# A two-layer hybrid trunk on one core: three weight copies placed behind the last scaled row of the feed-forward stage

## The chip, the cores and the metric

The kernel runs on one core of one Trainium2 chip. The metric is the device time of one execution in microseconds (us), the median of several runs. The core has five engines that each work through their own queue in order: PE (TensorE, matrix products), DVE (VectorE) and ACT (ScalarE) for elementwise work, POOL (GpSimd), and SP (SyncE), which here only issues transfers. They wait for one another through semaphores.

## What is computed

Two decoder layers on 528 columns (16 meta tokens and 512 tokens) of width 1024. Cut to what matters here:

```python
xn = rmsnorm(h, attn_norm_g)
proj = jnp.einsum('bld,dc->blc', xn, w_in)
...
mix = jnp.concatenate([fox_out, ret_out], axis=-1)
h = h + jnp.einsum('blc,cd->bld', mix, w_out)

hn = rmsnorm(h, ffn_norm_g)
ff = jax.nn.silu(jnp.einsum('bld,df->blf', hn, w_gate)) * jnp.einsum('bld,df->blf', hn, w_up)
return h + jnp.einsum('blf,fd->bld', ff, w_down)
```

All inputs and the output are float32. The second layer needs only the 512 token columns from the output projection on.

## The kernel before

Activations lie transposed: 8 tiles `h[0]` to `h[7]` of 128 rows (model width) by 528 columns. To keep precision, every operand of a product is written as a sum of two rounded parts, a high part (`xh`, `whi`, `fwhi`) that ACT copies and a low part (`xl`, `wlo`, `fwlo`) that DVE (or POOL) makes by subtracting; PE then does three products, high by high, high weight by low operand, low weight by high operand.

Weights come as jobs in a list. A job has a raw buffer (`raw`, a ring of four), filled by a transfer that SP issues; `convert` makes its high and low parts in halves of 128x512, into the ring `whi`/`wlo` (two deep) or, in the feed-forward stage, also into `fwhi`/`fwlo` (three deep).

The place that matters is the passage from the output projection to the feed-forward stage, once in each layer. It is made of these steps:

- The second half of the output projection makes eight results, one for each `h[m]`, by PE into PSUM (`psd` is a ring of two, `psa` another of four). DVE adds each to `h[m]` (`add_h`, lines 837 and 840). Results 4 and 5 use weights in `rqh`, `rql`, `rkh`, `rkl`; results 6 and 7 use weights in `whi`/`wlo`. Result 6 can begin only when DVE has emptied the `psd` buffer of result 4.
- `start_ffn` calls `scale_split`: for each k, ACT writes `xh[k]` from `h[k]` (line 347, "a scaled row" below) and DVE writes `xl[k]` (line 349). `squares` has ACT square each `h[k]` into `sq` (lines 360 and 365) and DVE sum them into `ss` (line 369). The sum of squares is split (`sqh`, `sql`), summed over the partitions by PE with a matrix of ones (line 310) and turned into the factor `R` (lines 315 to 327).
- The feed-forward stage has 22 blocks of 128 hidden columns. Blocks 0 and 1 are "plain": four dense products, gate 0, up 0, gate 1, up 1 (`dense_steps`, line 229). Gate 0 and both up products write `psd`, gate 1 writes `psa`. Their results are scaled by `R` on DVE (lines 878, 881, 889). Blocks 2 to 21 are "units" (`Unit`): a fast scheme with seven half-size products in place of eight. Their weights are made by `make1` to `make4` (lines 934, 935), and their operands `th`, `tl` by `x_forms` (lines 907 to 911, 153).
- The first three jobs of the stage are converted ahead of it: `start_ring` converts gate 0, `more_ring(1)` up 0, `more_ring(2)` gate 1. Up 1 (`whi`/`wlo`) and the first product of block 2 (`make1`) are converted by the steps that look ahead.

PE's order is written out by hand. ACT's, DVE's and POOL's orders are made by a scheduler from the program's order and priorities; `tc.issue_after(ins)` puts what is traced in its block behind `ins` on that engine, and `pin` keeps the written order. `ff["after"]` holds such marks for the jobs of the plain blocks: a dictionary, the key behind which the high copy goes (`"gated"`, the last gated retention result), and the key behind which the low copy goes.

Of the kernel before, what the change touches and what calls it, by code (L numbers as in the profile page):

```python
# [16 lines left out]
NK = D // 128  # L17
# [10 lines left out]
PLAIN = 2  # L28
# [11 lines left out]
def hybrid_kernel(ctx, tc, x_t, w_in, w_fl, w_out, w_gate, w_up, w_down, vecs, b_fg, rope, decay, mask, ident, out_t):  # L40
# [34 lines left out]
    def enter(name, side="left"):  # L75
        if side in phase:
            old, cm = phase.pop(side)
            cm.__exit__(None, None, None)
            phase.pop(old)
        if name:  # L80
            cm = tc.tile_pool(name=name, bufs=1, side=side, reuse_waits="tile")
            phase[side] = name, cm
            phase[name] = cm.__enter__()
# [91 lines left out]
    def convert(j, upto=NK, pinned=False):  # L175

        if j >= len(jobs):
            return
        job = jobs[j]
        fetch(j)  # L180
        if "make" in job:
            if "w" not in job:
                n = job["n"]
                hi, lo = (wring(job["ring"] + p) for p in ("whi", "wlo"))
                job["w"] = [(NK, hi, lo)]
                job["make"](hi[:, 0:n], lo[:, 0:n])
            return
        n = job["src"].shape[1]
        if "w" not in job:
            job["w"] = job["own"]() if job["own"] else \  # L190
                [(NK, *[wring(i) for i in ("whi", "wlo")])]
            job["split"] = 0
        sub = nc.gpsimd.tensor_sub if job["pool"] else nc.vector.tensor_sub
        while job["split"] < min(n, upto):
            c0 = job["split"]
            c1 = min(n, c0 + (2 if j < 2 and c0 < 4 else 4))
            size, hi, lo = job["w"][c0 // job["w"][0][0]]
            o = c0 % size
            hi, lo = hi[:, o:o + c1 - c0], lo[:, o:o + c1 - c0]
            marks, after, before = job["after"] or (None, None, None)  # L200
            with tc.high_priority() if j == 5 else tc.issue_after(marks[after]) if after else ExitStack():
                pin(nc.scalar.copy(hi, job["raw"][:, c0:c1]), pinned)  # L202
            step = 1 if job["pool"] else c1 - c0
            with tc.issue_after(marks[before]) if before else ExitStack():
                for c in range(0, c1 - c0, step):
                    pin(sub(lo[:, c:c + step], job["raw"][:, c0 + c:c0 + c + step], hi[:, c:c + step].bitcast(F32)), pinned)  # L206
            job["split"] = c1

    def dense_steps(src, parts, pool=False, banks=False, ahead=(1, 4), own=None, wait=None, far=False, after=None):

        j = len(jobs)
        jobs.append({"src": src, "pool": pool, "own": own, "after": after})

        def chunk(k0, k, n, xs, cols, ps, done):
            def go():
                convert(j)
                if k == 0:
                    t = [psum_a() for _ in cols] if banks else psum()  # L220
                    ps.append(t)
                    ps.append(t if banks else [t[:, b] for b in range(2)])
                size = jobs[j]["w"][0][0]
                _, hi, lo = jobs[j]["w"][(k0 + k) // size]
                wk = (k0 + k) % size
                xh, xl = xs(k)
                for i, (w, x) in enumerate(((hi, xh), (hi, xl), (lo, xh))):
                    for b, (c0, c1) in enumerate(cols):
                        nc.tensor.matmul(ps[1][b][:, 0:c1 - c0], w[:, wk, :], x[:, c0:c1],  # L229
                                         start=(k == 0 and i == 0), stop=(k == n - 1 and i == 2))  # L230
                if k == n - 1:
                    done(ps[0]) if wait is None else wait.append((ps[0], done))
                for half, at_step in enumerate(ahead):
                    if k0 + k == at_step:
                        convert(j + 1, 4 * half + 4)
                        if far:
                            convert(j + 2, 4 * half + 4)
            return go

        steps = []  # L240
        for k0, xs, n, cols, done in parts:
            ps = []
            steps += [chunk(k0, k, n, xs, cols, ps, done) for k in range(n)]
        return steps
# [28 lines left out]
    def psum_a():  # L273
        return psa.tile([128, 512], F32, name="psa", tag="psa")
# [64 lines left out]
    def scale_split(st, gcol, cols, then=None):  # L339

        c = slice(cols[0][0], cols[-1][1])
        st["x"] = []
        for k in range(NK):
            xh = state.tile([128, T], F32R, name=f"xh{k}", tag=f"xh{k}")
            xl = state.tile([128, T], F32R, name=f"xl{k}", tag=f"xl{k}")
            g = vcol(gcol + k)
            st["scaled"] = nc.scalar.activation(xh[:, c], h[k][:, c], AF.Copy, scale=g)  # L347
            pin(st["scaled"], then)
            pin(nc.vector.scalar_tensor_tensor(xl[:, c], h[k][:, c], g, xh[:, c].bitcast(F32),  # L349
                                               ALU.mult, ALU.subtract), then)  # L350
            st["x"].append((xh, xl))
            if then and k in then:
                then[k]()

# [503 lines left out]
    def ffn(l, st, real, last):  # L858
        QC = REAL if real else FULL
# [3 lines left out]
        xs = lambda k: st["x"][k]  # L863
# [22 lines left out]
        def u_done(f):  # L886
            def go(ps):
                u = tt("tq")
                nc.vector.scalar_tensor_tensor(sv(u, real), pv(ps, real), RSC, sv(st["R"], real), ALU.mult, ALU.mult)
                nc.vector.tensor_mul(sv(u, real), sv(u, real), sv(sgs[f], real))  # L890
                fh, fl = act_tile(f)
                split(sv(fh, real), sv(fl, real), sv(u, real))
                acts[f] = (fh, fl)
            return go
# [38 lines left out]
        def splits(hi, lo, src):  # L933
            nc.scalar.copy(hi, src)  # L934
            nc.vector.tensor_sub(lo, src, hi.bitcast(F32))  # L935
# [17 lines left out]
        class Unit:  # L953
# [17 lines left out]


            def make1(self, hi, lo):
                splits(hi, lo, self.t["a"])


            def make2(self, hi, lo):
# [123 lines left out]
        steps = []  # L1101
        fills = []
        units = {}
        for r, (f0, f1) in enumerate(ROUNDS):
            for f in range(f0, f1):
                if f < PLAIN:
                    if f == 0:
                        st["first"] = range(len(jobs), len(jobs) + 3)
                    steps += dense_steps(w_gate[l, f], [(0, xs, NK, QC, g_done(f) if f else held.append)], banks=f == 1, own=own, far=f == 1, after=st["after"][2 * f])
                    steps += dense_steps(w_up[l, f], [(0, xs, NK, QC, u_done(f))], own=None if f else own, far=f == 0, after=None if f else st["after"][1])  # L1110
                    continue
                for i in (f, f + 1) if f == PLAIN else (f,):
                    if i not in units:
                        units[i] = Unit(i)
                        steps += units[i].head()
                u = units[f]
                u.rest()
                steps += u.middle()
                p, g0, g1 = fills.pop(0)
                j = down_job(p, g0, g1)  # L1120
                steps += down(j, 0, 2 * p, g0, g1, not real or f < PLAIN + 2)
                u.last()
                steps += u.tail()
                steps += down(j, 1, 2 * p + 1, g0, g1, f == PLAIN)
            fills = [(p, f0, f1) for p in range(NK // 2)]
# [172 lines left out]
    def layer(l):  # L1298

        real = l == DEPTH - 1  # L1300
        QC = REAL if real else FULL
        ly, ff = {"wait": []}, {}
        fox = [{} for _ in range(FP)]
        ret = [{} for _ in range(RH)]
# [17 lines left out]
        plan = []  # L1322
# [34 lines left out]
        def more_ring(i):  # L1357
            return lambda: convert(ff["first"][i])
# [25 lines left out]
        plan = [lambda: enter_att(l), start]  # L1384
# [11 lines left out]
        for g in range(2):  # L1396
# [6 lines left out]
        op = out_proj(l, 0, mixes[0], real)  # L1403
# [6 lines left out]
        op = out_proj(l, 1, mixes[1], real, marks)  # L1410
# [1 line left out]
        plan += merge(base, spread(main, 2, 46.5), spread(rest, 51, 56),  # L1412
                      ret_places(2, 26, 23.5, 24.5, 32, 28, 33.5, 36, 56.5, 40.5, 57.5),
                      ret_places(3, 52, 45.5, 47.5, 57.5, 54.9, 58.5, 60, 64.1, 63, 64.2))
        plan += [start_ring, op[3], op[7], op[11], op[15]] + op[16:28] + [more_ring(1)] + op[28:] + [more_ring(2)]
        ff["after"] = [(ret[3], "gated", x) for x in ("mixed", ("added", 6), ("added", 7))]
        up = ffn(l, ff, real, real)
        plan += [lambda: enter("ffn"), start_ffn] + up
        return plan

    plan = [f for l in range(DEPTH) for f in layer(l)]
# [76 lines left out]
```

## Time and profile before

| | |
|---|---|
| median of 3 runs | 1269.51 us (1269.06 to 1270.74) |
| the profiled execution | 1271.65 us |
| its span, first to last instruction | 1269.9 us |
| granted TensorE clock, mean | 0.994 of full speed |
| transfers | 116.21 MB, 92 GB/s on average |
| passage of layer 0 / of layer 1 | about 266 to 314 us / about 893 to 944 us |

The profile is of one execution. Row by row, its timeline gives start, duration, engine, line, operation, output and inputs, how many instructions were merged into the row (x2), and in brackets the time that the engine sat idle just before, with what ended it. [...]

### The profile page before, as it was taken

The numbers are of one execution on the slowest core, as the hardware profiler recorded it, in microseconds if no ns is written. First come the engines' busy times: TensorE is split into PE (matmuls) and PEld (weight loads), VectorE is DVE, ScalarE is ACT, GpSimd is POOL, SyncE is SP. The second block draws the span as 40 slices with busy tenths as digits, with TensorE's granted clock in tenths as the row PEclk, the third lists the DMA queues.
The fourth block names the chain that finished last, engine by engine and source line by source line (L and its number), as shares of the span: only waits on it lengthen the run. The fifth ranks groups of instructions, "written<-read, shape, count | busy, mean of one in ns | idle before, by whom it ended". The sixth has DMA issues, their size and how long they took to land.

```text
span 1269.9 us, 23673 instructions
## 1 busy us (share of the span) xinstructions
PE 1251.1 (99%) x9291; PEld 1197.2 (94%) x9291; DVE 993.0 (78%) x1801; ACT 709.7 (56%) x1317; POOL 294.6 (23%) x568
## 2 busy tenths in 40 slices
PE   9999999999999999999999999999899999999997
PEld 8999999999999999999999988998789999999997
DVE  7887756889997777777776776468899978888866
ACT  7767656775544444444466675567655444444444
POOL 4545655430000000000045556655200000000000
PEclk9999999999999999999999999999899999999999
DMA  6222223123332333332312222222314333333312
GB/s 234 68 76 76 68 68 92 51 85 99 116 103 99 100 101 100 100 100 67 117 60 83 76 76 84 67 76 67 124 51 132 109 100 100 100 100 106 111 51 67
DMA packets 43344, 116.21 MB, mean 92 GB/s; under 512 B 5089, under 2 KB 9953, under 8 KB 43233
## 3 DMA queue, kind: packets, MB, share of 16 engines
q1 hardware_dynamic: 42800, 114.41, 28.0%
q8 instruction: 73, 1.20, 0.4%
q14 instruction: 39, 0.31, 0.1%
q10 hardware_dynamic: 432, 0.29, 0.1%
HBM read 112.58 MB, written 2.10 MB: 90 GB/s over the span
## 4 chain that ended last, share of the span: by engine, by line
PE 86%; DVE 7%; ACT 2%; POOL 2%; issue 2%; DMA 1%; DVEq 0%; POOLq 0%; ACTq 0%; SPq 0%
PE psd L229 23%; PE psa L946 19%; PE psd L946 14%; PE psd L1087 13%; PE psa L1087 5%; PE psa L229 3%; PE psa L449 2%; PE psa L616 2%; PE psa L546 1%; PE psa L750 1%; PE psa L786 1%; DVE ss L369 1%; DMA raw<-w_gate 1%; POOL rkl L206 1%; ACT xh L347 0%
## 5 line engine op out<-in xcount | busy, mean ns | idle before, releaser
L206 POOL TENSOR_TENSOR wlo<-raw,whi 128x128 fp32r<-128x128 f32 x488 | 254.7, 557 | 212.6 <-ACT whi L202 195.6
L229 PE MATMUL psd<-xh,whi 128*128 128x264 f32 (+1 forms) x696 | 169.5, 313 | 0.3 <-ACT whi L202 0.3
L229 PE MATMUL psd<-xh,wlo 128*128 128x264 f32 (+1 forms) x696 | 160.7, 300 | 0.0
L229 PE MATMUL psd<-xl,whi 128*128 128x264 f32 (+1 forms) x696 | 160.5, 299 | 0.2 <-DVE xl L349 0.2
L934 ACT CAST fwhi<-raw 128x1024 fp32r<-128x1024 f32 (+1 forms) x64 | 56.8, 889 | 108.3 <-PE psa L946 65.3
L229 PEld LDWEIGHTS psd<-xh,whi 128*128 128x128 f32 x696 | 112.1, 189 | 3.8 <-ACT whi L202 0.8
L229 PEld LDWEIGHTS psd<-xh,wlo 128*128 128x128 f32 x696 | 110.9, 188 | 4.4
L229 PEld LDWEIGHTS psd<-xl,whi 128*128 128x128 f32 x696 | 111.4, 188 | 3.0 <-DVE xl L349 0.4
L202 ACT CAST whi<-raw 128x512 fp32r<-128x512 f32 (+1 forms) x140 | 82.2, 612 | 32.8 <-PE psd L229 17.0
L125 POOL MEMSET kc<- 64x528 f32 x4 | 2.1, 534 | 377.2 <-PE psd L1087 377.1
L935 DVE TENSOR_TENSOR fwlo<-raw,fwhi 128x1024 fp32r<-128x1024 f32 (+1 forms) x64 | 65.2, 1018 | 30.6 <-ACT fwhi L934 30.6
L934 ACT CAST whi<-raw 128x1024 fp32r<-128x1024 f32 (+1 forms) x64 | 57.0, 890 | 43.5 <-PE psd L946 39.4
L935 DVE TENSOR_TENSOR wlo<-raw,whi 128x1024 fp32r<-128x1024 f32 (+1 forms) x64 | 65.2, 1019 | 8.1 <-ACT whi L934 8.1
L946 PE MATMUL psa<-tl,fwhi 128*128 128x264 f32 (+1 forms) x248 | 70.2, 283 | 0.0
L946 PE MATMUL psa<-th,fwhi 128*128 128x264 f32 (+1 forms) x248 | 70.2, 283 | 0.0
L946 PE MATMUL psa<-th,fwlo 128*128 128x264 f32 (+1 forms) x248 | 70.1, 283 | 0.0
L1014 ACT COPY e<-psa 128x264 f32<-128x264 f32 (+1 forms) x120 | 45.1, 376 | 40.9 <-PE psa L946 39.7
L946 PE MATMUL psa<-th,wlo 128*128 128x264 f32 (+1 forms) x232 | 66.1, 285 | 0.1
L946 PE MATMUL psa<-th,whi 128*128 128x264 f32 (+1 forms) x232 | 66.1, 285 | 0.0
L946 PE MATMUL psa<-tl,whi 128*128 128x264 f32 (+1 forms) x232 | 65.9, 284 | 0.0
L563 ACT ACTIVATE pr<-pr,nmax 128x144 f32<-128x144 f32 (+1 forms) x64 | 36.8, 576 | 45.7 <-DVE nmax L550 26.3
L934 ACT CAST whi<-S 128x1024 fp32r<-128x1024 f32 x22 | 23.1, 1049 | 66.0 <-PE psa L946 62.7
(411 smaller groups left out, 4221.8 us busy)
## 6 DMA issues: line engine op xcount, KB each, us to landing
raw<-w_in SPq DMA_DIRECT2D x54, 512.0 KB, 3.4
raw<-w_gate SPq DMA_DIRECT2D x44, 512.0 KB, 3.5
fraw<-w_up SPq DMA_DIRECT2D x40, 512.0 KB, 3.5
raw<-w_down SPq DMA_DIRECT2D x80, 256.0 KB, 3.4
raw<-w_out SPq DMA_DIRECT2D x16, 512.0 KB, 3.4
h<-x_t SPq DMA_DIRECT2D x8, 264.0 KB, 4.7
dec<-decay SPq DMA_DIRECT2D x8, 264.0 KB, 2.7
raw<-w_up SPq DMA_DIRECT2D x4, 512.0 KB, 4.1
```

The costliest lines, as they stand in the source:

```text
L202: pin(nc.scalar.copy(hi, job["raw"][:, c0:c1]), pinned)
L206: pin(sub(lo[:, c:c + step], job["raw"][:, c0 + c:c0 + c + step], hi[:, c:c + step].bitcast(F32)), pinned)
L229: nc.tensor.matmul(ps[1][b][:, 0:c1 - c0], w[:, wk, :], x[:, c0:c1], start=(k == 0 and i == 0), stop=(k == n - 1 and i == 2))
L369: nc.vector.tensor_add(acc[:, c], acc[:, c], sq[:, c])
L449: nc.tensor.transpose(ps[:, 128 * j:128 * j + 128], src[:, o:o + 128], idt)
L563: nc.scalar.activation(pr, pr, AF.Exp, bias=nmax[0:nq], scale=-1.0, accum_out=rsum)
L616: nc.tensor.matmul(po[:, c0:SEQ], v[:, j, :], pp[:, j, META + c0:T], start=(j == 0 and i == 0), stop=(j == 4))
L934: nc.scalar.copy(hi, src)
L935: nc.vector.tensor_sub(lo, src, hi.bitcast(F32))
L946: nc.tensor.matmul(bank()[:, 0:b.shape[-1]], a[:, o + k, :], b, start=(fresh and k == 0 and i == 0), stop=(k == n - 1 and i == 2), skip_gr ...
L1014: nc.scalar.copy(self.t["e"][:, i], self.t["x"][:, 0:w])
L1087: nc.tensor.matmul(v[:, 0:c1 - c0], a[:, s * n + k, :], b[:, c0:c1], start=(k == 0 and i == 0), stop=(k == n - 1 and i == 2))
```

## The change

Three weight jobs get another place on ACT (and, through what depends on them, on DVE): gate 1, up 1 ("the third and fourth plain block" of the four plain products) and the first product of block 2, the first unit. Their high copies are put behind the last scaled row, `xh[7]`. The call that converts gate 1 moves behind `start_ffn`, so that this mark exists when it is made.

```diff
@@ scale_split
             st["x"].append((xh, xl))
+            st["ready"] = st["scaled"].ins
@@ Unit
             def make1(self, hi, lo):
-                splits(hi, lo, self.t["a"])
+                with tc.issue_after(st["ready"]) if self.f == PLAIN else ExitStack():
+                    splits(hi, lo, self.t["a"])
@@ ffn, blocks 0 and 1
-                    steps += dense_steps(w_up[l, f], [(0, xs, NK, QC, u_done(f))], own=None if f else own, far=f == 0, after=None if f else st["after"][1])
+                    steps += dense_steps(w_up[l, f], [(0, xs, NK, QC, u_done(f))], own=None if f else own, far=f == 0, after=st["after"][1 + 2 * f])
@@ layer
-        plan += [start_ring, op[3], op[7], op[11], op[15]] + op[16:28] + [more_ring(1)] + op[28:] + [more_ring(2)]
-        ff["after"] = [(ret[3], "gated", x) for x in ("mixed", ("added", 6), ("added", 7))]
+        plan += [start_ring, op[3], op[7], op[11], op[15]] + op[16:28] + [more_ring(1)] + op[28:]
+        ff["after"] = [(ret[3], "gated", "mixed"), (ret[3], "gated", ("added", 6)), (ff, "ready", None), (ff, "ready", None)]
         up = ffn(l, ff, real, real)
-        plan += [lambda: enter("ffn"), start_ffn] + up
+        plan += [lambda: enter("ffn"), start_ffn, more_ring(2)] + up
```

No instruction is added or taken away. The orders of PE, SP and POOL stay as they are; ACT's and DVE's change in the two passages only.

ACT in layer 0, before, from the copies of gate 0, up 0 and gate 1 on (the six `fwhi` copies, two for each; `whi` 128x512 is up 1, `whi` 128x1024 the first unit; `h_73` to `h_80` are `h[0]` to `h[7]`):

```order
L202 CAST fwhi<-raw 128x512 x6
L347 ACTIVATE xh_4153<-h_73,vec 128x528
L360 ACTIVATE ss<-h_73 128x528
L347 ACTIVATE xh_4157<-h_74,vec 128x528
L347 ACTIVATE xh_4161<-h_75,vec 128x528
L347 ACTIVATE xh_4165<-h_76,vec 128x528
L365 ACTIVATE sq<-h_74 128x528
L365 ACTIVATE sq<-h_75 128x528
L365 ACTIVATE sq<-h_76 128x528
L202 CAST whi<-raw 128x512 x2
L347 ACTIVATE xh_4169<-h_77,vec 128x528
L365 ACTIVATE sq<-h_77 128x528
```

ACT in layer 0 after the change, at the other end of the same stretch, around the last scaled row (ahead of it stand `fwhi` x4 and then, with no weight copy between them, the other scaled rows and squares):

```order
L347 ACTIVATE xh_4169<-h_79,vec 128x528
L366 ACTIVATE sq<-h_79 128x528
L908 ACTIVATE S<-h_73,vec 128x528
L908 ACTIVATE S<-h_74,vec 128x528
L347 ACTIVATE xh_4173<-h_80,vec 128x528
L202 CAST fwhi<-raw 128x512 x2
L366 ACTIVATE sq<-h_80 128x528
L202 CAST whi<-raw 128x512 x2
L935 CAST whi<-raw 128x1024
L153 CAST sqh<-ss 128x528
L153 CAST th_4310<-S 128x1056
L935 CAST fwhi<-raw 128x1024
```

The two copies of gate 1 have gone from ahead of the first scaled row to behind the last, the two of up 1 from the middle to behind it, and that of the first unit from two rows ahead of it to four behind. In layer 1 it is the same, but for small swaps among rows that were free to run.

DVE in layer 0, from the addition of result 7 (`h_80`) on, before:

```order
L840 TENSOR_TENSOR h_80<-psd,h_80 128x528
L206 TENSOR_TENSOR fwlo<-raw,fwhi 128x512 x2
L206 TENSOR_TENSOR wlo<-raw,whi 128x512
L349 SCALAR_TENSOR_TENSOR xl_4182<-h_80,vec,xh_4181 128x528
L369 TENSOR_TENSOR ss<-ss,sq 128x528
L908 TENSOR_TENSOR S<-S 128x264
L910 SCALAR_TENSOR_TENSOR S<-h_77,vec,S 128x264 x2
L153 TENSOR_TENSOR sql<-ss,sqh 128x528
```

and after the change:

```order
L841 TENSOR_TENSOR h_80<-psd,h_80 128x528
L909 TENSOR_TENSOR S<-S 128x264
L911 SCALAR_TENSOR_TENSOR S<-h_77,vec,S 128x264 x2
L349 SCALAR_TENSOR_TENSOR xl_4174<-h_80,vec,xh_4173 128x528
L206 TENSOR_TENSOR fwlo<-raw,fwhi 128x512 x2
L370 TENSOR_TENSOR ss<-ss,sq 128x528
L206 TENSOR_TENSOR wlo<-raw,whi 128x512
L912 SCALAR_TENSOR_TENSOR S<-h_77,vec,S 128x264
```

The low copies of gate 1 and up 1 have moved behind the last low part `xl[7]`, and pieces of `x_forms` have moved ahead of it. Everything on DVE ahead of these rows stands as before.

## The prediction

> **What bounds the kernel now.** First the page's busy times and the list of what PE waited for (engine, output, releaser: us in total, times, longest).
>
> ```profile
> PE 1251.1 (99%) x9291; PEld 1197.2 (94%) x9291; DVE 993.0 (78%) x1801; ACT 709.7 (56%) x1317; POOL 294.6 (23%) x568
> ...
> PE psd L229 <- DVE h L840: 5.1, 2, 3.6
> PE psd L946 <- DVE tq L889: 1.9, 1, 1.9
> PE psa L1329 <- DVE wide L62: 1.6, 1, 1.6
> ```
>
> PE is busy all but 18.8 us of the span of 1269.9. No reordering on ACT and DVE can win more than those, and what a lowered clock costs inside the busy time. The two longest groups of waits, 7.0 us together, are on DVE; PE's timeline says that all three lie in the two passages into the feed-forward stage:
>
> ```profile
> 277.81 0.48 PE L229 MATMUL psd<-mxh,whi 128*128 128x264 f32 x2 [1.49 <-DVE h L840]
> ...
> 314.02 0.36 PE L946 MATMUL psd<-xh,fwhi 128*128 128x264 f32 x1 [1.86 <-DVE tq L889]
> ...
> 906.64 0.76 PE L229 MATMUL psd<-mxh,whi 128*128 128x512 f32 x1 [3.60 <-DVE h L840]
> ```
>
> The first and the third are result 6 of the output projection, which waits until DVE has taken result 4 out of its PSUM buffer, once in each layer. The second is the first product of unit 3, which waits until DVE has taken out up 1. Next, the view by stretches (start and length; busy us of PE, PEld, DVE, ACT, POOL; granted clock):
>
> ```profile
> 268.00:314.00 46.00, 42.67 (x349) 42.24 (x348) 43.38 (x73) 28.73 (x43) 0.00 (x0) 1.00 0.26 83
> 276.00:278.00 2.00, 0.51 (x4) 0.33 (x3) 1.66 (x4) 2.00 (x5) 0.00 (x0) 1.00 0.00 0
> 314.90:318.60 3.70, 3.70 (x20) 3.70 (x19) 3.70 (x7) 1.22 (x2) 0.00 (x0) 0.54 0.48 160
> 897.00:944.00 47.00, 43.28 (x200) 35.58 (x199) 41.07 (x67) 28.56 (x42) 0.00 (x0) 0.93 0.23 80
> 906.60:912.40 5.80, 5.76 (x14) 4.53 (x15) 5.15 (x9) 2.96 (x6) 0.00 (x0) 0.50 0.00 0
> ```
>
> In both passages DVE is the fullest engine: idle 46.00 - 43.38 = 2.62 us in layer 0 and 47.00 - 41.07 = 5.93 us in layer 1. And behind the waits of 1.86 and 3.60 us PE ran slowly: at 0.54 of its clock for 3.70 us (3.70 x 0.46 = 1.70 us lost) and at 0.50 for 5.80 us (2.9 us lost). The wait of 1.49 us left the clock at 1.00.
>
> Why was DVE idle? ACT and DVE of layer 0, from their timelines:
>
> ```profile
> 265.60 2.18 ACT L202 CAST fwhi<-raw 128x512 fp32r<-128x512 f32 x4
> 271.58 1.14 ACT L202 CAST fwhi<-raw 128x512 fp32r<-128x512 f32 x2 [3.80 <-DMA raw<-w_gate]
> 272.62 0.73 ACT L347 ACTIVATE xh<-h,vec 128x528 fp32r<-128x528 f32 x1
> ...
> 268.84 1.31 DVE L840 TENSOR_TENSOR h<-psd,h 128x528 f32<-128x528 f32 x2
> 270.07 1.43 DVE L837 TENSOR_TENSOR h<-psa,h 128x264 f32<-128x264 f32 x4
> 273.39 0.77 DVE L349 SCALAR_TENSOR_TENSOR xl<-h,vec,xh 128x528 fp32r<-128x528 f32 x1 [1.88 <-ACT xh L347]
> 274.55 1.45 DVE L349 SCALAR_TENSOR_TENSOR xl<-h,vec,xh 128x528 fp32r<-128x528 f32 x2 [0.40 <-ACT xh L347]
> 276.34 0.71 DVE L369 TENSOR_TENSOR ss<-ss,sq 128x528 f32<-128x528 f32 x1 [0.34 <-ACT sq L365]
> 276.96 0.70 DVE L840 TENSOR_TENSOR h<-psd,h 128x528 f32<-128x528 f32 x1
> ...
> 313.17 0.70 DVE L889 SCALAR_TENSOR_TENSOR tq<-psd,R 128x528 f32<-128x528 f32 x1
> ```
>
> ACT stands 3.80 us before the copies of gate 1, whose transfer has not landed, and the scaled rows stand behind them in ACT's queue. `h[0]` was ready at 268.84 + 0.70, about 269.5, but `xh[0]` starts at 272.62. DVE waits for it, and the addition at 276.96 on which PE waits stands in DVE's queue behind the low parts and a sum of squares. From 276.34 to the end of `tq` at 313.87 DVE never rests; 313.87 is what releases PE at 314.02. So **this DVE queue, fed late, sets the end of the passage**. In layer 1:
>
> ```profile
> 900.48 1.14 ACT L202 CAST fwhi<-raw 128x512 fp32r<-128x512 f32 x2 [5.14 <-DMA raw<-w_gate]
> ...
> 902.27 0.75 DVE L349 SCALAR_TENSOR_TENSOR xl<-h,vec,xh 128x512 fp32r<-128x512 f32 x1 [4.06 <-ACT xh L347]
> ...
> 904.54 0.69 DVE L369 TENSOR_TENSOR ss<-ss,sq 128x512 f32<-128x512 f32 x1 [0.25 <-ACT sq L365]
> ...
> 912.13 0.69 DVE L840 TENSOR_TENSOR h<-psd,h 128x512 f32<-128x512 f32 x1 [0.65 <-PE psd L229]
> ...
> 915.15 0.69 DVE L840 TENSOR_TENSOR h<-psd,h 128x512 f32<-128x512 f32 x1 [0.47 <-PE psd L229]
> ...
> 925.34 0.69 DVE L324 TENSOR_TENSOR nwt<-R 128x512 f32<-128x512 f32 x1 [0.50 <-ACT R L321]
> ...
> 942.55 1.23 DVE wlo L935
> 943.82 1.44 PE psa L946 x10
> ```
>
> The last two are from the chain of waits: PE's first product with a `th` operand follows DVE's `wlo` of unit 2. The two idles of 0.65 and 0.47 us are themselves made by the slow, late PE.
>
> **The change part by part.** It adds and removes no instruction; SP's, PE's and POOL's orders stay.
>
> *Gate 1's two copies leave the head of the scaled rows.* ACT need no longer stand for the transfer. `xh[0]` starts at about 269.5, some 3.1 us earlier; the squares follow. DVE's low parts are ready when DVE comes free (270.07 + 1.43 = 271.50), so its idles of 1.88, 0.40 and 0.34 us go: 2.62 us. Each idle also hid an overlap: the row at 270.07 starts 0.08 us before the one ahead ends (268.84 + 1.31). Three idles give 0.24 more, 2.9 us in all. The addition of result 4 then falls at about 276.96 - 2.9 = 274.1 and ends near 274.8, before PE needs the buffer (277.81 - 1.49 = 276.3): the wait of 1.49 us is gone. PE reaches unit 3 that much earlier, DVE releases it 2.9 us earlier, so what is left of the wait of 1.86 is 1.86 + 1.49 - 2.9 = 0.5 us. **Layer 0: 2.9 us from DVE.**
>
> *The slow clock.* With 0.5 us left the wait is shorter than that of 1.49, which left the clock at 1.00. So I take the 1.70 us of layer 0 as gone. [...]
>
> *Layer 1.* DVE's idles add to 4.06 + 0.25 + 0.65 + 0.47 + 0.50 = 5.93, plus five overlaps, 0.4. Is there any idle that comes in? PE would start result 6 at 906.64 - 3.60 = 903.04 without a wait and end result 7 some 24 products of 0.23 us later, near 908.6. DVE, without idles, reaches the addition of result 7 near 909.7, still behind PE. `xl[7]` must then wait for `xh[7]` (0.71 us on ACT) while DVE has one sum of squares of 0.6 us to do: about 0.2 us of idle. Net 6.1 us. PE's own side could give more (3.60 + 2.9 = 6.5), so DVE stays the limit. **Layer 1: 6.1 us**, the slow clock included.
>
> *Up 1's copies and the first unit's* leave the middle of the rows, 1.12 and 1.04 us of ACT. They add nothing to the sum: ACT is busy 28.73 of 46 us. Is gate 1 now too late?
>
> ```profile
> 296.00 0.41 PE L229 MATMUL psa<-xh,fwhi 128*128 128x264 f32 x2
> ...
> 286.82 0.72 ACT L347 ACTIVATE xh<-h,vec 128x528 fp32r<-128x528 f32 x1
> ...
> 292.81 0.40 PE L310 MATMUL psa<-sql,ones 128*128 128x264 f32 x2
> ...
> 290.70 0.69 DVE L153 TENSOR_TENSOR sql<-ss,sqh 128x528 fp32r<-128x528 f32 x1
> ```
>
> `xh[7]` was at 286.82 and comes at about 284. The two high copies take 1.14, the two low ones 1.28 us more: ready by 287. PE asks for gate 1 at 296.00 - 1.49 = 294.5: seven us of cover. The price if that cover were gone is PE's wait, one for one. The unseen costs, contention of the bunched copies with DVE and a longer `R` chain, I bound by 0 and by the 3.3 us of ACT work moved (1.14 + 1.12 + 1.04) in each layer; I take 0, as DVE's queue has no idle of ACT's making behind 276.34.
>
> *The sum*: 2.9 + 1.7 + 6.1 = 10.7 us. Against the profiled execution's own 1271.65 us that is 1260.95. The runs shown have their median at 1269.51, 2.14 lower, and spread over 1.68 us, about one slow stretch of 1.70. I read it so that the median run lacks the slow stretch of layer 0, which only just came about; it then has 10.7 - 1.7 = 9.0 us to win: **1260.5 us**.
>
> **The rivals.**
> *A constant distance*: the 2.14 us come from profiling, and the timed runs have both slow stretches. Then 1269.51 - 10.7 = 1258.8. For it: one profiled run proves no distance. Against it: the spread.
>
> *The bunch behind `xh[7]`*: 3.3 us of copies now stand ahead of `sqh` and `th` on ACT, and DVE waits for those. It would give back up to 3.3 us in each layer: 1260.5 + 6.6 = 1267.1 at the worst, 1264 in the middle. Against it: ACT has 17 us of idle in layer 0's passage.
>
> *It does nothing*: ACT is only one of two reasons, and PE then waits for the next thing late, result 5's addition or up 1's. Then 1267.5 to 1269.5. Against it: every idle of DVE ahead of 277 names ACT.
>
> *Slower: the sum of squares.* PE's order has the ones product inside up 0. `sql` was ready at 291.39 and PE used it at 292.81. PE comes 1.49 us earlier, at 291.3, and `sqh` now stands behind three sets of copies, `sql` behind four low ones. Worked from `xh[7]` at 284: 0.72 + 3.3 for the copies + 0.6 for `sq` + 0.63 for `sqh`, 289.3; `sql` done by 290. The slack is 1.3 us. From there each us late is a us of PE, with a slow clock behind it if it goes past 1.86. To be slower than before it would have to hold PE 5 us in each layer, and cost 2.9 of slow clock: 1269.5 + 3 = 1272.5. Nothing in the rows adds up to that.
>
> **How the numbers follow.** Forecast 1260.5 (own range 1259.5 to 1263): 0.50. Constant distance, 1258.8 (1257.5 to 1259.5): 0.25. The bunch, 1263 to 1267: 0.14. Nothing, 1267 to 1272: 0.07. Slower: 0.04. Within 0.2% (2.5 us) is about what a measurement of this kernel can't tell from no change. Faster by more: 0.50 + 0.25 + 0.14 = 0.89; same 0.07; slower 0.04. The range, 1257.5 to 1265, leaves out the two last cases and half of the bunch, 0.18.
>
> **What would show it.** Right: ACT's first scaled row near 269.5 and 897, no idle named for the transfer there; PE without a wait at results 6; the clock at 1.00 around both; about 0.5 us of wait left at unit 3, and as much in layer 1 at `wlo`. Wrong: a wait of PE on `sql`, `fwlo` or `R`; a lowered clock at a new place; DVE idle for `sqh` or `th`.

## The result, and the profile after

| | before | after |
|---|---|---|
| median of the runs | 1269.75 us (1269.06 to 1270.74, 6 runs) | 1260.57 us (1260.18 to 1261.29, 6 runs) |
| ratio, with its 95% interval | | 0.9928 [0.9915, 0.9941] |
| the profiled execution | 1271.65 us | 1260.22 us |
| its span | 1269.9 us | 1258.4 us |
| granted clock, mean | 0.994 | 0.998 |

The kernel became 9.2 us faster; 1260.5 had been forecast. The page after the change, its line of busy times:

```profile
PE 1245.6 (99%) x9291; PEld 1193.6 (95%) x9291; DVE 991.8 (79%) x1801; ACT 709.3 (56%) x1317; POOL 294.1 (23%) x568
```

and the list of what PE waited for (engine, output, releaser: us in total, times, longest):

```profile
PE psa L1331 <- DVE wide L62: 1.6, 1, 1.6
PE psd L947 <- DVE tq L890: 0.8, 1, 0.8
PE psa L617 <- DVE ptl L153: 0.6, 1, 0.6
PE psd L947 <- DVE h L1148: 0.5, 1, 0.5
PE psa L947 <- DVE wlo L936: 0.5, 1, 0.5
```

PE is busy 99% in both, so that share alone shows nothing. What shows the change is the list: the 5.1 us for `h` at result 6 (line 229) are gone, the 1.9 us for `tq` are 0.8, and `wlo` stands there with 0.5. (The 0.5 us for `h` at line 1148 stood there before the change too and lie behind the passages.) PE's busy time fell by 5.5 us with the same 9291 products; 4.6 of them agree with what the two slow stretches of before lost (3.70 x 0.46 and 5.80 x 0.50). The view by stretches of the two passages and of the places behind the former waits (start and length; busy us of PE, PEld, DVE, ACT, POOL; granted clock):

```profile
268.00:311.20 43.20, 42.40 (x349) 42.22 (x348) 43.20 (x73) 28.73 (x43) 0.00 (x0) 1.00 0.28 97
313.00:317.00 4.00, 4.00 (x36) 4.00 (x35) 4.00 (x7) 2.47 (x4) 0.00 (x0) 1.00 0.44 141
897.00:938.00 41.00, 40.51 (x223) 34.84 (x222) 40.80 (x67) 26.74 (x41) 0.00 (x0) 1.00 0.25 84
903.00:910.00 7.00, 7.00 (x32) 5.70 (x31) 6.80 (x12) 5.78 (x11) 0.00 (x0) 1.00 0.69 248
```

DVE is never idle in the passage of layer 0 (43.20 of 43.20 us) and idle 0.20 us in that of layer 1. The clock is 1.00 in all four. In this whole execution it is low only from 1254 us to the end (0.50), behind PE's last product; that is why the mean is 0.998 and not 1. Now the rows of layer 0: first ACT at the head of the scaled rows and at the last of them, then DVE, then PE at unit 3.

```profile
264.80 2.18 ACT L202 CAST fwhi<-raw 128x512 fp32r<-128x512 f32 x4
268.77 0.74 ACT L347 ACTIVATE xh<-h,vec 128x528 fp32r<-128x528 f32 x1 [1.80 <-DVE h L841]
...
282.87 0.74 ACT L347 ACTIVATE xh<-h,vec 128x528 fp32r<-128x528 f32 x1 [0.59 <-DVE h L841]
283.52 1.13 ACT L202 CAST fwhi<-raw 128x512 fp32r<-128x512 f32 x2
...
268.04 1.31 DVE L841 TENSOR_TENSOR h<-psd,h 128x528 f32<-128x528 f32 x2
269.27 1.44 DVE L838 TENSOR_TENSOR h<-psa,h 128x264 f32<-128x264 f32 x4
270.63 2.11 DVE L349 SCALAR_TENSOR_TENSOR xl<-h,vec,xh 128x528 fp32r<-128x528 f32 x3
272.67 0.70 DVE L370 TENSOR_TENSOR ss<-ss,sq 128x528 f32<-128x528 f32 x1
273.28 0.70 DVE L841 TENSOR_TENSOR h<-psd,h 128x528 f32<-128x528 f32 x1
...
288.03 0.69 DVE L153 TENSOR_TENSOR sql<-ss,sqh 128x528 fp32r<-128x528 f32 x1
...
309.49 0.70 DVE L890 SCALAR_TENSOR_TENSOR tq<-psd,R 128x528 f32<-128x528 f32 x1
...
310.33 0.36 PE L947 MATMUL psd<-xh,fwhi 128*128 128x264 f32 x1 [0.80 <-DVE tq L890]
```

ACT waits for no transfer any more: the first scaled row waits for DVE's own addition, and starts when `h[0]` is there. DVE goes from its additions straight on to the low parts. The two runs are best compared from one common row, DVE's first addition (268.84 before, 268.04 after), since the start of the passage differs by 0.80 us between these two executions, and lies between 268.0 and 269.3 in those of all kernels here. From it, the addition of result 4 came 8.12 us later before and 5.24 after; `tq` 44.33 and 41.45. Both are 2.88 us earlier. And in layer 1:

```profile
891.76 0.73 ACT L347 ACTIVATE xh<-h,vec 128x512 fp32r<-128x512 f32 x1 [1.72 <-DVE h L841]
...
891.05 1.27 DVE L841 TENSOR_TENSOR h<-psd,h 128x512 f32<-128x512 f32 x2
892.25 0.67 DVE L838 TENSOR_TENSOR h<-psa,h 128x512 f32<-128x512 f32 x1
892.84 0.74 DVE L349 SCALAR_TENSOR_TENSOR xl<-h,vec,xh 128x512 fp32r<-128x512 f32 x1
...
905.60 0.75 DVE L349 SCALAR_TENSOR_TENSOR xl<-h,vec,xh 128x512 fp32r<-128x512 f32 x1 [0.20 <-ACT xh L347]
...
932.40 0.39 PE L947 MATMUL psa<-th,wlo 128*128 128x256 f32 x1 [0.49 <-DVE wlo L936]
```

The first low part follows DVE's first addition after 1.79 us. The 0.20 us at `xl[7]` are the only idle left on DVE.

Below, "the passage" is the time from DVE's first addition to PE's first down product (the first with `ah` and `whi`), which cuts off what happens elsewhere:

| profiled execution of | layer 0 | layer 1 |
|---|---|---|
| before | 52.62 us | 51.60 us |
| after | 48.22 us | 45.46 us |
| gain | 4.40 us | 6.14 us |

Between the passages lie 574.88 us before and 574.79 after, and from the end of the second one to PE's last row 312.18 and 312.17. So the 11.43 us between the two profiled executions are 4.40 and 6.14 from the passages, 0.80 from the start, and 0.1 from the rest.

### The profile page after: what moved, and what is told of

Read it like the earlier page. It is cut to its first block, busy times and chain, and to the rows that moved or that the text cites. A ratio compares the mean times of both kernels' runs of the same rounds, so it can differ in the third digit from the quotient of the medians.

```text
span 1258.4 us, 23677 instructions
## 1 busy us (share of the span) xinstructions
PE 1245.6 (99%) x9291; PEld 1193.6 (95%) x9291; DVE 991.8 (79%) x1801; ACT 709.3 (56%) x1317; POOL 294.1 (23%) x568
## 4 chain that ended last, share of the span: by engine, by line
PE 85%; DVE 10%; ACT 1%; DMA 1%; issue 1%; DVEq 0%; SPq 0%
PE psd L229 23%; PE psa L947 19%; PE psd L947 14%; PE psd L1089 13%; PE psa L1089 5%; PE psa L229 3%; PE psa L450 2%; PE psa L617 2%; PE psa L547 1%; PE psa L751 1%; PE psa L787 1%; DMA raw<-w_in 1%; DVE ss L370 1%; DVE tl L153 1%; DVE xl L349 1%
```

## The experiments

Two theories were set against each other first. One: the transfer at the head of ACT's scaled rows starves DVE and, through it, PE. The other: the moved copies themselves, or the first unit's and up 1's places, make the gain. The runs of before beside them had medians of 1269.5 to 1269.9 us.

**Gate 1 alone.** The changed kernel, with up 1's and the first unit's copies where they stood before:

```diff
             def make1(self, hi, lo):
-                with tc.issue_after(st["ready"]) if self.f == PLAIN else ExitStack():
-                    splits(hi, lo, self.t["a"])
+                splits(hi, lo, self.t["a"])
...
-    after=st["after"][1 + 2 * f]
+    after=None if f else st["after"][1]
```

> Only gate 1's copies are put behind the last scaled row; up 1's and the first unit's stay where they were, in the middle of the rows. Theory A (the gain is that ACT no longer stands for gate 1's transfer ahead of the scaled rows): nearly the whole gain of the change, 8 to 9.5 us below the kernel before, PE without a wait at result 6 in both layers, DVE idle under 0.6 us in either passage. Theory B (the gain comes from clearing the 2.2 us of other copies out of the rows): less than half, under 4.5 us.

1261.65 us (1261.17 to 1262.16), ratio 0.9933 [0.992, 0.9945]: 8.1 us below before, most of the gain. The passage of layer 0 is 48.23 us, as after the whole change; that of layer 1 is 46.54, 1.1 us longer. The timelines of ACT, DVE and PE in layer 1 say why:

```profile
898.94 1.14 ACT L202 CAST whi<-raw 128x512 fp32r<-128x512 f32 x2 [1.64 <-DMA raw<-w_up]
...
905.66 1.03 ACT L935 CAST whi<-raw 128x1024 fp32r<-128x1024 f32 x1
906.98 0.72 ACT L347 ACTIVATE xh<-h,vec 128x512 fp32r<-128x512 f32 x1 [0.28 <-DVE h L841]
...
901.26 0.69 DVE L370 TENSOR_TENSOR ss<-ss,sq 128x512 f32<-128x512 f32 x1 [1.16 <-ACT sq L366]
...
934.35 0.38 PE L947 MATMUL psa<-th,wlo 128*128 128x256 f32 x1 [0.91 <-DVE wlo L936]
```

Up 1's copies, left in the middle of the rows, there wait 1.64 us for their own transfer: the same fault, smaller. DVE stands 1.16 us for the squares behind them, where under 0.6 had been expected, and PE's wait at `wlo` grows from 0.49 to 0.91. The first unit's copy has no part in it: it ends before `h[7]` is there, and ACT still waits 0.28 us for DVE behind it. Moving gate 1 is most of the change; moving up 1 is worth about 1 us, in layer 1 only.

**Up 1 and the first unit alone.** Before, with only the other two moves:

```diff
+            st["ready"] = st["scaled"].ins
...
-                splits(hi, lo, self.t["a"])
+                with tc.issue_after(st["ready"]) if self.f == PLAIN else ExitStack():
+                    splits(hi, lo, self.t["a"])
...
-    after=None if f else st["after"][1]
+    after=(st, "ready", None) if f else st["after"][1]
```

> The other half of the change alone: up 1's and the first unit's copies behind the last scaled row, gate 1's at the head as before. Theory A: within 1.5 us of the kernel before, ACT idle 3.8 and 5.1 us before gate 1's copies as before, PE waiting 1.5 and 3.6 us at result 6 (up to 0.5 us less, as ACT's rows in the middle come a little earlier), the slow clock still there in layer 1. Theory B: 4 to 9 us faster.

1269.33 us (1267.27 to 1271.23, 11 runs), ratio 0.9993 [0.9984, 1.0002]: no difference. The waits are nearly those of before, as ACT's and PE's timelines show:

```profile
270.69 1.14 ACT L202 CAST fwhi<-raw 128x512 fp32r<-128x512 f32 x2 [3.60 <-DMA raw<-w_gate]
...
313.14 0.36 PE L947 MATMUL psd<-xh,fwhi 128*128 128x264 f32 x1 [1.91 <-DVE tq L890]
904.21 0.47 PE L229 MATMUL psd<-mxh,whi 128*128 128x512 f32 x1 [3.58 <-DVE h L841]
```

and this is the view by stretches around PE's two waits and behind them:

```profile
312.00:318.00 6.00, 4.86 (x40) 4.89 (x41) 6.00 (x11) 1.89 (x4) 0.00 (x0) 1.00 0.58 183
902.00:908.00 6.00, 3.79 (x17) 3.12 (x18) 5.89 (x10) 4.22 (x8) 0.00 (x0) 1.00 0.00 0
```

What is missing there is the slow clock. PE waits 1.91 and 3.58 us, close to before (1.86 and 3.60), but the clock stays at 1.00, in layer 1 against the expectation. This execution took 1267.27 us, the lowest of the kernel's runs. Its passages of 50.91 and 49.65 us are 1.71 and 1.95 shorter than those of before. In layer 0 a part of that is not the clock: ACT stood 3.60 us for the transfer in place of 3.80, and unit 3's first product came 44.99 us behind DVE's first addition in place of 45.18. Without these 0.19 us, 1.52 are left. In layer 1 ACT stood as long as before (5.15 and 5.14 us). So one slow stretch costs 1.52 us in layer 0 and 1.95 in layer 1 at the end of the passage. What the change gains apart from the clock is then 4.40 - 1.52 = 2.88 us in layer 0 and 49.65 - 45.46 = 4.19 us in layer 1.

The 11 runs of this one kernel go up in steps of about that size: three at a mean clock of 0.997 or 0.998 took 1267.3 to 1267.5 us, seven at 0.995 or 0.996 took 1269.0 to 1269.9, and one at 0.994 took 1271.2.

**No transfer to wait for, everything else as before.** Gate 1's copies read gate 0's raw buffer. Gate 1's own transfer is left out, so block 1 works with gate 0's weights:

```diff
+        elif job.get("lend"):
+            job["raw"] = jobs[j - 2]["raw"]
...
+                    jobs[-1]["lend"] = f == 1
```

> The order of before, gate 1's copies still at the head of the scaled rows, but they read gate 0's raw buffer, which landed earlier; gate 1's own transfer is left out, so block 1 of each layer uses gate 0's weights in place of its own. Theory A (the transfer is what costs, not the copies): ACT starts the copies at once, they fit into the 1.7 us in which it has no scaled row ready anyway, and the gain is 7.5 to 9.5 us. Theory C (copies ahead of the rows cost by their own time, 1.1 us in each layer, with what follows): no more than 5 us of gain, PE still waiting 0.5 us or more at result 6 in both layers.

1268.64 us (1266.66 to 1269.75, 11 runs), ratio 0.9987 [0.9979, 0.9996]: not the gain that was expected, and no verdict on either theory. The scheduler, with gate 1 free, had moved one of up 1's copies ahead of the first scaled row, and that one waited instead, 2.48 us in layer 0 and 4.05 in layer 1. In layer 0:

```profile
266.09 3.22 ACT L204 CAST fwhi<-raw 128x512 fp32r<-128x512 f32 x6
271.80 0.62 ACT L204 CAST whi<-raw 128x512 fp32r<-128x512 f32 x1 [2.48 <-DMA raw<-w_up]
272.32 1.37 ACT L349 ACTIVATE xh<-h,vec 128x528 fp32r<-128x528 f32 x2
```

**The same, with the other two sets tied behind `xh[7]`.** So up 1's copies can't step into the gap: the edit of the run before together with that of "up 1 and the first unit alone". Gate 1's copies stay at the head, ahead of all scaled rows; only what they wait for is gone.

> As the run with up 1's and the first unit's copies alone behind the last scaled row, in the same order on DVE and, but for one pair, on ACT; gate 1's copies stand at the head of the scaled rows. The one difference: they read gate 0's raw buffer, gate 1's transfer is left out and block 1 of each layer uses gate 0's weights. No other weight copy stands ahead of the scaled rows, so no other transfer can be waited for there. Theory A (the transfer costs, not the copies): ACT reaches the first scaled row by about 0.2 us behind h[0], PE doesn't wait at result 6, 8 to 9.5 us below the kernel before, the passages 48 to 48.6 us and 45.4 to 46.2 us long (from the first addition of the passage to the first down product; 52.6 and 51.6 before). Theory C (the copies' own 1.1 us at the head cost): passages at least 1 us longer than after the change in each layer.

1261.09 us (1260.65 to 1261.22), ratio 0.9933 [0.992, 0.9945]. ACT at the head of the scaled rows, layer 0 and layer 1:

```profile
265.16 3.22 ACT L204 CAST fwhi<-raw 128x512 fp32r<-128x512 f32 x6
269.13 0.74 ACT L349 ACTIVATE xh<-h,vec 128x528 fp32r<-128x528 f32 x1 [0.75 <-DVE h L843]
...
888.31 3.22 ACT L204 CAST fwhi<-raw 128x512 fp32r<-128x512 f32 x6
892.22 0.73 ACT L349 ACTIVATE xh<-h,vec 128x512 fp32r<-128x512 f32 x1 [0.68 <-DVE h L843]
```

All six copies run at one go and still end 0.7 us before the first scaled row can begin. The passages are 48.21 and 45.29 us, as after the change (48.22, 45.46). So the two copies cost nothing at that place: what cost time was the transfer behind them. The first theory holds, and the rival falls.

**Filling PE's wait in layer 1**, to learn what the slow clock alone costs: 13 products that nobody reads, ahead of result 6.

```diff
+        def fill():
+            if l == DEPTH - 1:
+                ps = psum_a()
+                for _ in range(13):
+                    nc.tensor.matmul(ps, ones, mixes[1][0]["mix"][0][:, META:T], start=True, stop=True)
...
-    ... + op[16:28] + ...
+    ... + op[16:24] + [fill] + op[24:28] + ...
```

> The kernel before, with 13 products of 512 columns (3.0 us) whose result nobody reads put into PE's wait of 3.60 us at result 6 of layer 1. Nothing is taken off the wait itself. If the wait lowers the clock: no slow stretch behind it (clock 1.00 from 903 to 912), PE reaches gate 0 2.5 to 3 us earlier, and the passage's end, which DVE sets, comes 1.0 to 2.0 us earlier: 1.0 to 2.0 us below the kernel before. If the slow stretch has another cause, the clock is 0.50 there as before, and the time is the same.

1270.8 us (1269.51 to 1271.0, 11 runs), ratio 1.0005 [0.9996, 1.0013]. The stretch of result 6 and the one behind it:

```profile
902.00:906.00 4.00, 3.57 (x16) 2.62 (x15) 3.74 (x7) 4.00 (x9) 0.00 (x0) 1.00 0.02 6
906.00:912.00 6.00, 5.62 (x24) 4.22 (x23) 6.00 (x11) 2.76 (x5) 0.00 (x0) 1.00 0.00 0
```

The clock stayed at 1.00, and none of the 11 runs has a mean clock of 0.995 or less, as 28 of the 45 runs of before beside these experiments have. So the fill kept the clock up. Yet the passage took 51.31 us, hardly less than the 51.60 of before: the scheduler had also put up 1's low copies ahead of result 6's addition on DVE, and PE got new waits, 1.01 us for that addition and 1.40 for `tq`. As to the price of a slow stretch the run is inconclusive; that rests on "up 1 and the first unit alone".

**Gate 1's low copies on POOL.** If DVE's queue is what sets the end, the 1.28 us of these two copies, in each layer, might go to the idle POOL. The changed kernel and:

```diff
+                    jobs[-1]["pool"] = f == 1
```

> The changed kernel, with gate 1's two low copies per layer on POOL, which is idle there, as eight pieces of about 0.56 us. If DVE's queue still sets the end of the passages, 1.2 us leave it and the rest of PE's waits (0.8 us at the product of unit 3 in layer 0, 0.5 us at wlo in layer 1) go: 0.8 to 1.3 us faster than the changed kernel. If POOL slows DVE while both work (DVE's copy pair took 1.82 us beside POOL and 1.28 us alone), the same 4.5 us of POOL cost DVE up to 1.5 us and nothing is won.

1263.06 us (1262.79 to 1263.69), ratio to before 0.995 [0.9936, 0.9963]: 2.5 us slower than the change, where at the worst no gain had been expected. POOL and DVE in layer 0, then in layer 1:

```profile
284.74 9.21 POOL L206 TENSOR_TENSOR fwlo<-raw,fwhi 128x128 fp32r<-128x128 f32 x8 [17.24 <-ACT fwhi L202]
...
287.71 1.52 DVE L153 TENSOR_TENSOR tl<-S,th 128x1056 fp32r<-128x1056 f32 x1
289.15 0.96 DVE L153 TENSOR_TENSOR sql<-ss,sqh 128x528 fp32r<-128x528 f32 x1
290.91 1.48 DVE L936 TENSOR_TENSOR wlo<-raw,whi 128x1024 fp32r<-128x1024 f32 x1
...
907.60 5.20 POOL L206 TENSOR_TENSOR fwlo<-raw,fwhi 128x128 fp32r<-128x128 f32 x8 [14.71 <-ACT fwhi L202]
...
908.61 0.91 DVE L370 TENSOR_TENSOR ss<-ss,sq 128x512 f32<-128x512 f32 x1 [0.81 <-ACT sq L366]
```

POOL takes 9.21 / 8 = 1.15 us for each of eight pieces in layer 0 and 5.20 / 8 = 0.65 in layer 1, against 0.56 on the mean of its 488 in the changed kernel. DVE's rows beside it take 1.52, 0.96 and 1.48 us in layer 0, where the same rows of the changed kernel take 1.24, 0.69 and 1.21. In layer 1 DVE, without the two low copies to do, also stands 0.81 us until ACT has made a square behind gate 1's copies. The passage of layer 0 gained 0.3 us (47.93), that of layer 1 lost 1.2 (46.62), and 1.2 us more went between the passages, for a reason that was not looked into.

**The two waits that are left.** The wait of 0.80 us at unit 3 is on DVE's `tq`, which stands in DVE's queue behind two low copies of 1.22 us each. A higher priority for it when up 1 is taken out:

```diff
-                nc.vector.scalar_tensor_tensor(sv(u, real), ...)
+                with tc.high_priority() if f else ExitStack():
+                    nc.vector.scalar_tensor_tensor(sv(u, real), ...)
```

> The changed kernel, with the operation that takes up 1 out of PSUM ahead of four others on DVE. If its place in DVE's queue is what makes PE wait 0.8 us at unit 3 in layer 0, that wait goes and layer 0's passage is 0.6 to 0.8 us shorter; layer 1's stays as it is, to 0.2 us. If DVE is behind as a whole, the wait only moves to the next DVE product and the passage keeps its length.

1260.07 us (1259.62 to 1260.74), ratio to before 0.9926 [0.9911, 0.9941]. The passage of layer 0 is 47.23 us, 1.0 shorter, and `tq` is gone from PE's waits; layer 1 is unchanged (45.48) and keeps 0.5 us at `wlo`. The median shows only 0.5 us of it: in the profiled execution 0.3 us more went between the passages (575.12 us against 574.79). Then, besides, the third product's copies of unit 2 behind those of its second, so that `wlo` isn't pushed back:

```diff
-                    splits(hi, lo, s)
+                    self.second = splits(hi, lo, s)
...
-                    splits(hi, lo, b)
+                    with tc.issue_after(self.second[0]) if self.f == PLAIN else ExitStack(), tc.issue_after(self.second[1]) if self.f == PLAIN else ExitStack():
+                        splits(hi, lo, b)
```

> The run before this one, and the third product's copies of unit 2 behind those of its second, which PE needs first. If the place in the queue is what counts, PE's wait of 0.5 us at wlo in layer 1 goes as well: 1.0 to 1.3 us faster than the changed kernel, with both passages 0.5 to 0.8 us shorter. If DVE is behind as a whole, no more than 0.3 us.

1259.41 us (1259.27 to 1260.21), ratio 0.9922 [0.9908, 0.9935]; passages 47.18 and 44.95. Both versions were then run once more side by side on one chip, the changed kernel first:

> The changed kernel once more, beside the further version on one chip. 1260 to 1261.5 us; every timed execution at a mean clock of 0.998 or more, while those of the kernel before spread from 0.994 to 0.998 with the time falling as the clock rises (theory: the slow clock behind its waits comes in some executions only, none is left after the change). If the slow clock has nothing to do with the waits, the changed kernel's clock spreads as much.

> The version with up 1 taken out early and the second product's copies first, once more. Both of PE's last waits are gone from it, so 1.0 to 1.6 us faster than the changed kernel on the same chip; passages near 47.2 and 45.0 us. If the difference seen was between chips, the two medians lie within 0.4 us.

The changed kernel: 1260.6 us (1260.54 to 1261.38), ratio 0.9929 [0.9917, 0.9942], with passages of 48.22 and 45.48 us, as the first time. The further one: 1259.09 (1259.07 to 1259.42), ratio 0.9917 [0.9903, 0.993], so 1.5 us below it, and the two ranges don't touch. What PE waits for in the further one:

```profile
PE psa L1332 <- DVE wide L62: 1.6, 1, 1.6
PE psa L617 <- DVE ptl L153: 0.8, 2, 0.6
PE psd L947 <- DVE h L1149: 0.5, 1, 0.5
PE psd L229 <- DVE xl L349: 0.2, 1, 0.2
```

`tq` and `wlo` are gone from it; the longest waits that are left lie outside the passages. By the intervals against before alone the two versions overlap; it is the runs side by side that part them.

## Why the prediction was right, point by point

*DVE's queue, fed late, sets the end of the passage*: shown. Take the transfer away from the kernel of "up 1 and the first unit alone", with all else in place, and both passages are as short as after the change (48.21 and 45.29 us).

*Layer 0, 2.9 us from DVE*: 2.88 us at the addition of result 4, and still 2.88 at `tq`. Nothing that DVE had gained was lost on the way, as the step had it. *The first scaled row near 269.5 and 897*: 268.77 and 891.76. In layer 0 that is 0.73 us behind the first addition's start, as forecast (269.5 less 268.84 is 0.7); in layer 1 the 897 holds only on the old time scale, for by then the run was 5.3 us ahead (891.05 against 896.34).

*The wait at result 6 goes*: yes, in both layers. *0.5 us left at unit 3*: 0.80. PE reached result 6 at 275.31, 7.27 us behind the first addition; the sum had 276.32 - 268.84 = 7.48. So 0.2 of the 0.3 us is PE's being early.

*The slow stretch of layer 0, 1.7 us*: it is gone, and was worth 4.40 - 2.88 = 1.52 us at the end of the passage; the run that had the waits without the slow clock gives the same. The term was 0.2 us too large.

*Layer 1, 6.1 us, the slow clock included*: 6.14. The run without it splits this into 4.19 from DVE and 1.95 from the clock. The 0.2 us of new idle at `xl[7]` came as worked out (0.20), and so did the wait at `wlo` (0.49).

*Up 1's and the first unit's copies add nothing*: this step was mis-sized. Without those two moves layer 1 is 1.1 us longer, by up 1's. ACT's share of busy time was the wrong thing to argue from: up 1's copies wait for their own transfer (1.64 us) once gate 1's wait no longer covers it. It didn't show in the sum, since the sum for layer 1 was made as if DVE would find no idle at all, which is true only with up 1 moved as well.

*The sum, 10.7 us*: the two passages gave 4.40 + 6.14 = 10.54. The profiled execution fell by 0.9 more, of which 0.80 is its earlier start, which nobody forecast and which varies by 1.3 us among the profiles here.

*The median run lacks one slow stretch*: right in kind. 45 runs of before, taken beside the experiments, go with their mean clock: 5 runs at 0.998 took 1268.2 us on the mean, 22 at 0.995 took 1270.1, 6 at 0.994 took 1270.9. The changed kernel had 0.998 or 0.999 in all 11 of its runs. So most runs of before have one stretch or so, few have none or both. Of the 9.2 us, 2.88 + 4.19 = 7.1 us come from DVE being fed earlier, and the other 2.1 us agree with one stretch (1.52 or 1.95) and a little. That it is layer 0's stretch which the median run lacks was only argued, and remains open; so that the forecast came within 0.1 us of the median is in part luck.

*The rivals.* Constant distance: fell. Before, the profiled execution was 1.9 us above the median of the six runs; after, it is 0.35 below (1260.22 against 1260.57). The bunch behind `xh[7]`: fell. DVE has no idle for `sqh` or `th`. It does nothing: fell by the ratio. The sum of squares: `sql` was done at 288.03 + 0.69 = 288.72, and PE didn't wait for it.

## What to carry to other kernels

An in-order engine that feeds another should not have, at the head of the work that the other waits for, an instruction that waits for a transfer, however cheap it is: two copies of 0.57 us cost 2.9 and 4.2 us here, through the 3.80 and 5.14 us that ACT stood before them. When such a wait is removed, look which transfer is late next in the same queue, since the wait ahead of it had covered it (up 1's, 1.64 us, where gate 1 alone was moved). To price an idle on the engine that sets the end, sum its idles with their overlaps (0.08 us where DVE's row at 270.07 starts before the one ahead ends) from its own timeline and carry the sum to the next place where the bound engine waits for it; it held here to 0.1 us in both layers.

## What the runs showed of the hardware

**The clock falls behind a wait in some executions and not in others.** Behind waits of 1.86 and 3.60 us the granted clock was 0.54 and 0.50 for 3.70 and 5.80 us in the profiled execution of before; behind 1.91 and 3.58 us in the one of "up 1 and the first unit alone" it stayed at 1.00, while other runs of that kernel had mean clocks down to 0.994. In two more profiles, those of the first run without the transfer and of the filled wait, the clock fell behind waits of 1.88 and 1.85 us at unit 3 (0.83 from 310 to 320 us in both). One such stretch cost 1.52 and 1.95 us at the end of the passage. So a wait of PE has two prices, its own length and, in some executions, a slow stretch. The length of the wait alone does not part the cases: the clock fell behind 1.86 us and stayed at 1.00 behind 1.91 and 3.58. What does part them was not shown.

**POOL's and DVE's rows were longer where both worked.** With gate 1's low copies on POOL, DVE's rows beside them in layer 0 took 0.96 us in place of 0.69, 1.48 in place of 1.21 and 1.52 in place of 1.24. POOL's subtractions of 128x128 took 1.15 us on the mean there and 0.65 in layer 1, against 0.56 on the mean of the 488 in the changed kernel.
